# A token-major residual stream for a two-layer diffusion backbone: 512-column output products, a norm turned by a diagonal product, gates broadcast from DRAM

## The chip, the cores and the metric

The kernel runs on one core of a Trainium2 chip. The metric is the device time of one execution in microseconds (us), the median of several runs. Inputs and weights lie in DRAM; all weights, some 590 MB with the modulation matrices, are read once per execution.

## The reference, cut to what matters

Two groups of 128 tokens, a prompt and a latent sample, pass through two layers of width 2048 with the same weights. Each layer normalises and modulates its input, runs three mixers on one input projection, and adds the gated output projection; then it does the same with a SwiGLU feed-forward part. The modulation vectors come from a product of a condition vector with `w_mod`, per layer six of 2048 columns, and each group has its own. The change touches the norms, the two gated residual sums and the end.

```python
def rms_norm(x, g):
    y = x * lax.rsqrt(jnp.mean(x * x, axis=-1, keepdims=True) + EPS)
    return y * g

def trunk_layer(x, mod, lp, ctx=None):
    sh1, sc1, g1, sh2, sc2, g2 = [m[:, None] for m in jnp.split(mod, 6, axis=-1)]
    h = rms_norm(x, lp['ln_mix']) * (1.0 + sc1) + sh1
    u_hy, u_gla, u_mla = _split(h @ lp['w_in'], (HY_IN, GLA_IN, MLA_IN))
    ...
    y = jnp.concatenate([y_hy, y_gla, y_mla], axis=-1) @ lp['w_out']      # 2048 x 2048
    x = x + g1 * y
    h = rms_norm(x, lp['ln_ffn']) * (1.0 + sc2) + sh2
    gate, up = jnp.split(h @ lp['w_ffn_in'], 2, axis=-1)                  # 2048 x 2*5632
    x = x + g2 * ((jax.nn.silu(gate) * up) @ lp['w_ffn_out'])             # 5632 x 2048
    return x, ...

# both groups, layers 0 and 1, then
y_prompt, y_sample = rms_norm(x_ctx, ln_final), rms_norm(x_lat, ln_final)
```

## The kernel before, in words

**Products.** All large products run in a split form: every fp32 weight tile `w` of 128 rows and up to 1024 columns is rounded by ScalarE to a high part `wh` (`act`, L157) and VectorE makes the low part `wl = w - wh` (`tt`, L130); activations have a high and a low part too, and three products of TensorE (`mm`, L166) stand for one. `gemm_steps` walks over the row tiles of a weight; `weights` loads a tile on SP's DMA queue and splits it, one step ahead. A plan says what a step multiplies. A "w" entry (`plan_w`) holds a 128x128 piece of the weight still and moves the 256 tokens past it, so the result is feature-major: features on partitions, tokens along the columns. A "t" entry holds 128 tokens of the activation still and moves up to 512 weight columns past it, so the result is token-major. `w_in`, `w_out` and `w_ffn_out` use "w" entries (apart from two of the gated linear attention); `w_ffn_in` uses "t" entries. Four PSUM banks (`ps_g`) take the result. After the last `tail` row tiles, done bank by bank, `evict` drains each bank.

**The residual stream** `xT` is feature-major, 16 tiles of 128 features by 256 tokens. At the start x is loaded token-major and turned by 32 transposes. `residual` adds a bank into it with four VectorE operations of 128 columns (the gate of a feature is a per-partition number of `modv`). `SquareSum` squares two tiles at a time on ScalarE, adds most of them on VectorE and sums over partitions by products with a matrix of ones, the last ones right after the last banks. `rsq` turns that into the inverse root `rstd`, 256 columns wide on every partition. `norm_mod`'s `pre(k)` makes one tile of the normalised input, high and low, from `xT` and `rstd`; it is called in the step that uses tile k, so the mixer's first product (`c_a`) and the FFN's first product come with it. At the end `final_transpose` and `final_scale` turn x back and scale it.

**Order.** Tile's list scheduler orders each engine's instructions; program order is the priority. `w_mod` columns (`mods`) are computed beside the rest: layer 0's first two by TensorE in four quarters during the start (`mod_first`), others by `mod_pe` (TensorE) or `mod_dve` (VectorE sums `macc`, L295, ticked per product step). `early_load`/`early_run` put a few row tiles of the next modulation product into TensorE's waits at the end of `w_out` and of layer 0's `w_ffn_out`. VectorE's sums emitted after a product are ordered behind the last vector operation of its eviction (`dve["evict"]`).

**FFN.** Three segments of 16, 16 and 12 column tiles of 128. In a segment `w_ffn_in` runs gate, then up, for 8 (last segment: 6) column tiles at a time; `turn` transposes the result (L1210) and splits it into `ah`, `al`; then `w_ffn_out` runs twice, for 1024 output columns each (r = 0, 1). `w_out` runs twice in the same way.

## Time and profile before

| | us |
|---|---|
| median of 3 runs | 2466.58 (2464.02 to 2468.85) |
| the profiled execution | 2465.36 |
| its span, first to last instruction | 2463.3 |

| stage of the span | us | TensorE busy | VectorE busy |
|---|---|---|---|
| w_out, layer 0, until its modulation sums end (435 to 513) | 78.00 | 74.84 | 77.76 |
| FFN's first steps with the norm (543 to 591) | 48.00 | 48.00 | 47.87 |
| w_ffn_out, second segment, layer 0 (993 to 1085) | 92.00 | 92.00 | 83.59 |
| w_ffn_out, first segment, layer 1 (1878 to 1971) | 93.00 | 93.00 | 46.97 |

Matmuls overlap: an instruction's duration runs from its start to the end of its last column, and the next one starts long before that. The pace of TensorE is the distance of starts. An fp32 product (not the rounded form) leaves two records, a transpose one. TensorE's granted clock is 1.00 in all of these stages.

### The profile page before, as it was taken

The numbers are of one execution on the slowest core, as the hardware profiler recorded it, in microseconds if no ns is written. First come the engines' busy times: TensorE is split into PE (matmuls) and PEld (weight loads), VectorE is DVE, ScalarE is ACT, GpSimd is POOL, SyncE is SP. The second block draws the span as 40 slices with busy tenths as digits, with TensorE's granted clock in tenths as the row PEclk, the third lists the DMA queues.
The fourth block names the chain that finished last, engine by engine and source line by source line (L and its number), as shares of the span: only waits on it lengthen the run. The fifth ranks groups of instructions, "written<-read, shape, count | busy, mean of one in ns | idle before, by whom it ended". The sixth has DMA issues, their size and how long they took to land.

```text
span 2463.3 us, 39715 instructions
## 1 busy us (share of the span) xinstructions
PE 2400.4 (97%) x15925; PEld 2093.2 (85%) x15925; DVE 1725.8 (70%) x2439; ACT 1027.9 (42%) x1413; POOL 0.2 (0%) x4
## 2 busy tenths in 40 slices
PE   6899999999999999999999999999999999999998
PEld 3567777988889888999997888998888988899998
DVE  3565555988888978888988565698696555454555
ACT  2234342445433434434445444335443344434443
POOL 0000000000000000000000000000000000000000
PEclk9999999999999999999999999999999999999999
DMA  8988887877777878777876676586785666656662
GB/s 300 321 288 308 292 298 270 299 240 244 252 272 264 291 261 302 241 266 260 316 293 181 226 248 214 182 301 218 246 282 186 187 191 188 193 181 169 186 203 95
DMA packets 167276, 600.73 MB, mean 244 GB/s; under 512 B 18576, under 2 KB 24882, under 8 KB 146612
## 3 DMA queue, kind: packets, MB, share of 16 engines
q1 hardware_dynamic: 164104, 592.27, 71.4%
q10 hardware_dynamic: 2988, 5.93, 0.7%
q8 instruction: 125, 2.05, 0.3%
q14 instruction: 59, 0.48, 0.1%
HBM read 592.03 MB, written 6.09 MB: 243 GB/s over the span
## 4 chain that ended last, share of the span: by engine, by line
PE 90%; DMA 4%; DVE 4%; ACT 1%; issue 1%; SPq 0%; ACTq 0%; DVEq 0%
PE pg L166 77%; PE px L166 8%; DMA mw<-in_w_mod_dram 4%; PE mps L166 3%; DVE macc L295 2%; DVE wl L130 1%; PE px L1210 1%; DVE xT L135 0%; DVE sqa L130 0%; DMA w<-in_w_in_dram 0%; ACT e L157 0%; PE px L955 0%; ACT wh L157 0%; DVE nt L135 0%; PE px L984 0%
## 5 line engine op out<-in xcount | busy, mean ns | idle before, releaser
L157 ACT ACTIVATE wh<-w 128x1024 fp32r<-128x1024 f32 (+3 forms) x816 | 768.2, 950 | 1118.8 <-PE pg L166 931.7
L130 DVE TENSOR_TENSOR wl<-w,wh 128x1024 fp32r<-128x1024 f32 (+3 forms) x816 | 873.0, 1086 | 479.6 <-ACT wh L157 472.2
L166 PE MATMUL pg<-wh,hh 128*128 128x512 f32 (+1 forms) x1600 | 597.5, 374 | 1.1 <-DVE nt L135 1.1
L166 PE MATMUL pg<-wh,hl 128*128 128x512 f32 (+1 forms) x1600 | 596.0, 372 | 0.0
L166 PE MATMUL pg<-wl,hh 128*128 128x512 f32 (+1 forms) x1600 | 594.9, 372 | 0.0
L295 DVE SCALAR_TENSOR_TENSOR macc<-mw,sc,macc 128x1024 f32<-128x1024 f32 x324 | 402.0, 1280 | 0.0
L166 PE MATMUL pg<-ah,wh 128*128 128x256 f32 x1408 | 397.4, 283 | 0.0
L166 PE MATMUL pg<-al,wh 128*128 128x256 f32 x1408 | 396.3, 282 | 0.0
L166 PE MATMUL pg<-ah,wl 128*128 128x256 f32 x1408 | 395.4, 281 | 0.0
L166 PEld LDWEIGHTS pg<-wh,hh 128*128 128x128 f32 x1600 | 300.5, 188 | 45.0 <-ACT hh L157 2.9
L166 PEld LDWEIGHTS pg<-wl,hh 128*128 128x128 f32 x1600 | 300.5, 188 | 42.6
L166 PEld LDWEIGHTS pg<-wh,hl 128*128 128x128 f32 x1600 | 300.8, 188 | 41.2 <-issue 0.3
L166 PEld LDWEIGHTS pg<-ah,wh 128*128 128x128 f32 x1408 | 265.2, 189 | 1.8 <-issue 1.7
L166 PEld LDWEIGHTS pg<-al,wh 128*128 128x128 f32 x1408 | 265.7, 189 | 0.2
L166 PEld LDWEIGHTS pg<-ah,wl 128*128 128x128 f32 x1408 | 265.5, 189 | 0.1
L166 PE MATMUL pg<-hh,wh 128*128 128x256 f32 x832 | 245.0, 296 | 4.1 <-ACT hh L157 2.1
L166 PE MATMUL pg<-hl,wh 128*128 128x256 f32 x832 | 239.3, 289 | 0.0
L166 PE MATMUL pg<-hh,wl 128*128 128x256 f32 x832 | 236.2, 287 | 2.5 <-DVE wl L130 2.4
L166 PEld LDWEIGHTS pg<-hh,wh 128*128 128x128 f32 x832 | 159.7, 192 | 31.6 <-issue 19.5
L166 PEld LDWEIGHTS pg<-hl,wh 128*128 128x128 f32 x832 | 159.9, 192 | 10.0 <-issue 8.7
L166 PEld LDWEIGHTS pg<-hh,wl 128*128 128x128 f32 x832 | 158.6, 192 | 11.3 <-issue 6.3
L166 PE MATMUL mps<-mw,sc 128*32 128x256 f32 (+1 forms) x1024 | 113.8, 522 | 21.2 <-DMA mw<-in_w_mod_dram 21.0
(289 smaller groups left out, 2155.1 us busy)
## 6 DMA issues: line engine op xcount, KB each, us to landing
mw<-in_w_mod_dram SPq DMA_DIRECT2D x160, 1024.0 KB
w<-in_w_ffn_in_dram SPq DMA_DIRECT2D x256, 512.0 KB
w<-in_w_ffn_out_dram SPq DMA_DIRECT2D x176, 512.0 KB
w<-in_w_ffn_in_dram SPq DMA_DIRECT2D x128, 384.0 KB
mw<-in_w_mod_dram SPq DMA_DIRECT2D x64, 512.0 KB
w<-in_w_in_dram SPq DMA_DIRECT2D x64, 512.0 KB
w<-in_w_out_dram SPq DMA_DIRECT2D x64, 512.0 KB
w<-in_w_in_dram SPq DMA_DIRECT2D x64, 256.0 KB
```

Of the source, the lines that this page charges most:

```text
L130: r = nc.vector.tensor_tensor(out=out, in0=a, in1=b, op=op)
L157: r = nc.scalar.activation(out=out, in_=a, func=func, **k)
L166: r = nc.tensor.matmul(*args, **kw)
L295: r = nc.vector.scalar_tensor_tensor(out=acc[:, i, cs], in0=w[:, cs], scalar=c, in1=acc[:, i, cs], op0=ALU.mult, op1=ALU.add)
L1210: nc.tensor.transpose(p[:, j], s[:, 128 * j:128 * j + 128], ident)
```

## The change

The residual stream becomes `xt`, token-major: 128 tokens on partitions, 2048 features along the columns, one half per group. x is loaded straight into it.

- `w_out` and `w_ffn_out` use "t" entries: a step is 12 products of 512 columns (`plan_t`) and not 24 of 256. The last FFN segment takes 8 and then 4 column tiles; for the 4, gate and up share one product.
- `residual` multiplies a bank with the gate (`tt`, 512 columns) and adds it (`tt`). The gate must now lie along the columns, the same on all partitions: `mod_finish` transposes a finished gate, copies it to SBUF and stores it in DRAM on POOL's queue; `gate_load` reads it back with a partition broadcast, 2 x 512 KB ahead of each product.
- `square` sums squares along the columns by ScalarE's accumulator; `token_rms` turns them into one factor per token and a diagonal matrix `diag`.
- `norm_mod` multiplies a 128x128 tile of `xt` with `diag` (fp32, two products per k): that turns the tile and scales it at once. Scale and shift are applied on the way out of PSUM. `gemm_steps` calls `pre` one step ahead (`LOOK`).
- After `w_out` the early products are put ahead of the flush of the modulation sums.
- At the end no transposes: ln_final is read by partition broadcast and multiplied, and `scale_out` scales and sends each group.

```diff
+    def gate_load(l, m, r, pool, tags):
+        out = []
+        for g, tag in enumerate(tags):
+            t = pool.tile([128, 1024], F32, tag=tag, name="gb", bufs=1)
+            src = gates[l, m].rearrange("(g h k) c -> g h (k c)", g=2, h=2)[g, r]
+            nc.gpsimd.dma_start(t, src.partition_broadcast(128))
+            out.append(t)
+        return out
...
+    def square(pool, tag, g, j, bufs):
+        junk = pool.tile([128, 512], F32, tag=tag, name="junk", bufs=bufs)
+        act(junk, xt[:, g, 512 * j:512 * j + 512], AF.Square, accum_out=ssq[:, g, j:j + 1])
+
+    def token_rms(g, final=False):
+        m, r, t = (ssq[:, g, 4 + i:5 + i] for i in range(3))
+        nc.vector.tensor_reduce(out=m, in_=ssq[:, g, 0:4], axis=mybir.AxisListType.X, op=ALU.add)
+        ts(m, m, 1.0 / D, ALU.mult, EPS, ALU.add)
+        act(r, m, AF.Ln)
+        act(r, r, AF.Exp, scale=-0.5)
+        stt(t, m, r, r, ALU.mult, ALU.mult)
+        ts(t, t, -0.5, ALU.mult, 1.5, ALU.add)
+        if final:
+            tt(t, t, r, ALU.mult)
+            return t
+        ts(diag[:, g], ident, r, ALU.mult, t, ALU.mult)
...
         def pre(k):
+            p = px([128, 2, 128])
+            for g in range(2):
+                mm(p[:, g], xt[:, g, 128 * k:128 * k + 128], diag[:, g], start=(g == 0), stop=(g == 1))
             t = pool.tile([128, 256], F32, tag="nt", name="nt", bufs=2)
             for g in range(2):
                 s = slice(g * 128, g * 128 + 128)
-                b = modv[:, l, msh, k, g:g + 1]
-                stt(t[:, s], xT[:, k, s], modv[:, l, msc, k, g:g + 1], rstd[:, s], ALU.mult, ALU.mult)
-                act(hh[:, k, s], t[:, s], AF.Identity, bias=b)
-                stt(hl[:, k, s], t[:, s], b, hh[:, k, s].bitcast(F32), ALU.add, ALU.subtract)
+                c, b = modv[:, l, msc, k, g:g + 1], modv[:, l, msh, k, g:g + 1]
+                act(hh[:, k, s], p[:, g], AF.Identity, scale=c, bias=b)
+                ts(t[:, s], p[:, g], c, ALU.mult, b, ALU.add)
+            tt(hl[:, k], t, hh[:, k].bitcast(F32), ALU.subtract)
...
+    def residual(pool, tag, bufs, gb, b, r, bank, squares):
+        g, i = divmod(b, 2)
+        j = 2 * r + i
+        x = xt[:, g, 512 * j:512 * j + 512]
+        t = pool.tile([128, 512], F32, tag=tag, name="rt", bufs=bufs)
+        tt(t, bank, gb[g][:, 512 * i:512 * i + 512], ALU.mult)
+        tt(x, x, t, ALU.add)
+        if squares:
+            square(pool, tag, g, j, bufs)
+        return g, j
...
+    plan_t = [(2 * t + i, 0, 512, f"t{t}", 512 * i) for t in range(2) for i in range(2)]
...
-                gemm([T["w_out"][l][:, 1024 * r:1024 * r + 1024]], k_tiles(order), yT, plan_w(8), ev_out, tail=1 + r, quiet=QUIET * r,
+                gemm([T["w_out"][l][:, 1024 * r:1024 * r + 1024]], k_tiles(order), yT, plan_t, ev_out, tail=1 + r, quiet=QUIET * r,
                      done=(lambda: early_run(l, 5, range(1), pe["last"])) if r else None)
+            early_run(l, 5, range(1, EARLY), pe["last"])
             mod_flush((l, 3))
-            early_run(l, 5, range(1, EARLY), pe["last"])
-            rsq(rstd, ss.ps, ss.acc[:, 0:256])
...
-                    n = 8 if nkt == 16 else 6
+                    n = min(8, nkt - done_kt)
...
+                    if n == 8:
+                        run_late(gemm_steps([w_gate], k_tiles(range(KT)), hT, plan, ev_gate_ff, pre=pre, quiet=16 if pre else 0))
+                        run_late(gemm_steps([w_up], k_tiles(range(KT)), hT, plan, ev_up))
+                    else:
+                        run_late(gemm_steps([w_gate, w_up], k_tiles(range(KT)), hT, plan, ev_both))
```

## Rows read from the trace of the kernel before

**Rows 1.** The page: busy time of each engine; shares of the chain that ended last.
```profile
PE 2400.4 (97%) x15925; PEld 2093.2 (85%) x15925; DVE 1725.8 (70%) x2439; ACT 1027.9 (42%) x1413; POOL 0.2 (0%) x4
...
PE 90%; DMA 4%; DVE 4%; ACT 1%; issue 1%; SPq 0%; ACTq 0%; DVEq 0%
```
**Rows 2.** Timeline of TensorE, w_ffn_in and w_ffn_out: start us, us, instruction, count.
```profile
654.64 0.39 PE L166 MATMUL pg<-wh,hh 128*128 128x512 f32 x1
...
656.90 0.39 PE L166 MATMUL pg<-wh,hl 128*128 128x512 f32 x1
...
1039.74 0.28 PE L166 MATMUL pg<-al,wh 128*128 128x256 f32 x1
...
1041.50 0.28 PE L166 MATMUL pg<-al,wh 128*128 128x256 f32 x1
```
**Rows 3.** Chain in order of time, FFN of layer 0: start us, us, what, count.
```profile
639.54 2.76 PE pg L166 x12
...
1002.20 0.44 PE px L1210 x4
1002.64 2.82 PE pg L166 x24
...
1160.76 2.09 PE pg L166 x12
```
**Rows 4.** Timeline of TensorE, fp32 products of 128 columns in the Hyena mixer.
```profile
395.95 0.39 PE L166 MATMUL px<-mats,yim 128*128 128x128 f32 x2
...
396.85 0.39 PE L166 MATMUL px<-mats,yim 128*128 128x128 f32 x2
```
**Rows 5.** Stretches: us, each engine's busy (instructions), granted clock, DMA share, GB/s.
```profile
435.00:513.00 78.00, 74.84 (x617) 72.70 (x616) 77.76 (x91) 33.49 (x37) 0.00 (x0) 1.00 0.85 306
...
543.00:591.00 48.00, 48.00 (x212) 39.72 (x213) 47.87 (x89) 29.79 (x52) 0.00 (x0) 1.00 0.65 210
993.00:1085.00 92.00, 92.00 (x786) 91.96 (x785) 83.59 (x95) 35.08 (x36) 0.00 (x0) 1.00 0.77 264
...
1878.00:1971.00 93.00, 93.00 (x789) 92.61 (x782) 46.97 (x61) 34.84 (x35) 0.00 (x0) 1.00 0.58 181
45.00:60.00 15.00, 12.89 (x111) 9.12 (x110) 8.47 (x29) 6.12 (x17) 0.00 (x0) 0.92 0.76 257
```
**Rows 6.** Chain, from w_out to the FFN in layer 0.
```profile
534.50 5.23 PE px L166 x20
...
542.99 3.04 PE pg L166 x12
```
**Rows 7.** Chain, from layer 0's w_ffn_out to layer 1.
```profile
1294.15 1.12 DVE xT L135 x4
1295.27 4.79 DVE macc L295 x4
...
1301.17 3.41 PE mps L166 x26
```
**Rows 8.** Chain, the first norm of layer 0.
```profile
44.06 3.62 PE px L166 x8
...
51.17 1.93 PE pg L166 x12
```
**Rows 9.** Chain, the end.
```profile
2449.23 0.44 PE px L984 x4
...
2456.48 1.33 DVE yt L140 x2
```
**Rows 10.** Squares of x: ns min/median/max, first and last start us, shapes.
```profile
L157 ACT ACTIVATE sq<-xT x35: 613/630/636, 37.8 to 2451.8; 128x512 f32<-128x512 f32 x35
...
L130 DVE TENSOR_TENSOR sqa<-sqa,sq x22: 649/692/695, 38.4 to 2444.4; 128x512 f32<-128x512 f32 x22
```
**Rows 11.** One-column operations of the attention's softmax, same columns.
```profile
L157 ACT ACTIVATION_READ_ACCUMULATOR e<-px,st x32: 192/204/217, 216.9 to 1445.5; 128x1 f32 x32
L140 DVE TENSOR_SCALAR st<-st x16: 158/162/171, 216.2 to 1444.2; 128x2 f32<-128x2 f32 x16
```

More of the change, by code (lines that the diff above doesn't have):

```diff
@@ L40 @@
 EARLY = 4
+LOOK = 1
 FF_RATE = 0.252
@@ L235, in mod_finish @@
         mods_done.add((l, m))
+        if m in (2, 5):
+            p = px([32, 128])
+            nc.tensor.transpose(p, modv[:, l, m].rearrange("p k g -> p (k g)"), ident)
+            row = mp.tile([32, 128], F32, tag="mtr", name="row", bufs=1)
+            act(row, p)
+            gates[l, m] = dram.tile([32, 128], F32, name=f"gate{l}{m}")
+            nc.gpsimd.dma_start(gates[l, m], row)
     def mod_load(l, m, kt, pool):
@@ L384, in gemm_steps @@
         for ti, (row, kt) in enumerate(tiles):
+            if pre is not None:
+                for i in range(0 if ti == 0 else ti + LOOK, min(ti + LOOK + 1, nt)):
+                    pre(tiles[i][1])
             fetch(ti + 1)
             wh, wl = ahead.pop(0)
-            if pre is not None:
-                pre(kt)
             a, c = x(kt)
@@ L558, in tile_backbone @@
         nc.vector.tensor_copy(out=v2T, in_=p[:, :at])
[L560 to L581 removed]
+        for g, nm in enumerate(("x_prompt", "x_sample")):
+            for half in range(2):
+                cs = slice(half * 1024, half * 1024 + 1024)
+                nc.scalar.dma_start(xt[:, g, cs], T[nm][0, :, cs])
+        for g in range(2):
+            for j in range(4):
+                square(pool, "junk", g, j, 2)
+            token_rms(g)
     def hyena_filters(pool, l):
@@ L812, in gla @@
             p = px([128, 2, 2, 128])
-            mm(p, ones[:, 3], sq, start=True, stop=True)
+            mm(p, ones[:, 2], sq, start=True, stop=True)
             rsq(sq, p, og[:, g].rearrange("p (i j) t -> p i j t", i=2))
@@ L1205, in turn @@
                             halves[half] = ah, al
[L1206 to L1209 removed]
+                            parts.extend((ah[:, j], al[:, j]) for j in range(4))
+                        ah, al = (v[:, :, 128 * t:128 * t + 128] for v in halves[half])
+                        p = px([128, 4, 128])
+                        for j in range(4):
                             nc.tensor.transpose(p[:, j], s[:, 128 * j:128 * j + 128], ident)
@@ L1243, in tile_backbone @@
                         early_load(l + 1, 4)
-                    run_late(gemm_steps([T["w_ffn_out"][l][:, 1024 * r:1024 * r + 1024]], tiles, aT, plan_w(8), ev_ff, tail=2 if last_seg and r else 1,
+                    run_late(gemm_steps([T["w_ffn_out"][l][:, 1024 * r:1024 * r + 1024]], tiles, aT, plan_t, ev_ff, tail=2 if last_seg and r else 1,
                          quiet=QUIET if nxt else 0,
```

154 lines of the change are left out of this document (45 added, 109 removed).

## Prediction

> **What bounds the kernel now.** I read the page's engine totals and its chain first. TensorE is busy 97% of the span and 90% of the chain that ended last lies on it [rows 1], so what counts is TensorE's issue time, stage by stage, and then the few places where TensorE waits. Busy durations mislead here, because matmuls overlap, so I took starts from the timeline: ten 512-column products of w_ffn_in start 2.26 us apart in all, 0.226 each, and fifteen 256-column products of w_ffn_out 1.76 us apart, 0.117 each [rows 2]. Two 256-column products cost 0.235, one 512-column product 0.226: the half-width form is only some 4% dearer, although its recorded duration is 0.28 against 0.39. The chain in order of time says the same with small additions: 24 narrow products in 2.82, 12 wide ones in 2.76, 12 of 384 columns in 2.09 [rows 3].
>
> The table of stretches then shows who limits each stage [rows 5]. In w_out (435 to 513) VectorE is busy 77.76 of 78 us: there TensorE waits for VectorE. In w_ffn_out of layer 0 VectorE has 83.59 of 92 us, near the limit; in layer 1 only 46.97 of 93.
>
> **The change part by part.** All sums are made against the profiled execution (2465.36 us, span 2463.3; it is 1.22 below the median of the runs).
>
> *w_ffn_out, wide.* 44 row tiles x 2 column halves x 2 layers = 176 steps, each 24 narrow products before and 12 wide ones after. A step now: the stretch 993 to 1085 holds 32 steps and four groups of transposes at 0.44 [rows 3], (92 - 1.8)/32 = 2.82; 1878 to 1971 gives (93 - 1.8)/32 = 2.85 [rows 5]. Mean 2.835. After: 12 x 0.226 to 0.227 = 2.72. 176 x 0.115 = 20 us less. The low end is the chain's pair, 2.82 against 2.76, 176 x 0.06 = 10.6; I take 20, because the pieces of the chain begin and end at transposes and the stretches don't. [...] Each bank is now drained by two 512-element tensor_tensor (0.69 recorded, [rows 10]) in place of four 128-element operations (1.12 for four, [rows 7]): 0.25 us more per bank, on VectorE, beside the next product. For layer 0, where VectorE has 8 us of slack in 92 and TensorE takes away 4, I charge 2 us. Net -18.
>
> *w_ffn_in's last segment.* Four products of 16 steps x 12 x 384 columns become three of 16 x 12 x 512: 64 x 2.09 = 133.8 against 48 x 2.74 = 131.5 [rows 2, 3]. -2.3 per layer, -4.6.
>
> *w_out.* Until 513 VectorE decides, and what it does there is mostly weight splitting and the modulation sums, both unchanged. Its drain of four banks goes from 1.12 + 0.62 (the sum of squares moves away) to 1.3: -1.8 us. Past 513 seven steps are left at -0.115: -0.8. One ones-product group (0.9) leaves TensorE. -3.5 per layer; the gate copies add 2 MB to a stage whose DMA share is already 0.85 [rows 5], which I charge with 1 us (0 to 3, if they displace weight loads one for one). -2.5 per layer, -5.
>
> *Norm by a diagonal product.* This is the added cost. Each of 16 k needs two fp32 products of 128 columns. The nearest row is in the Hyena inverse transform: fp32 128x128 products start 0.22 us apart, and each appears as two records [rows 4]. 16 x 2 x 0.223 = 7.1 us per norm, 7.4 with the change of operand type around it. Before, the norm had nothing on TensorE. In both FFN norms and in layer 1's mixer norm the products that follow are limited by TensorE, so three norms are paid in full: +22. The look-ahead of one step hides the ScalarE and VectorE part, not this. From below: if TensorE had waits there to fill it would be less, but in 543 to 591, the norm's stretch, TensorE is busy 48.00 of 48 us [rows 5], so I exclude a gain.
>
> *Layer 0's start and mixer norm.* The x transposes go (hidden anyway). The chain from the sum of squares to the first product is ones-product 3.62, then rstd and norm until 51.17 [rows 8]; after it, squares and row factors can be ready as soon as x lands, and the first product waits for the modulation columns at about 44.1, so it starts some 5 us earlier. Bytes bound the stage: DMA runs at 257 GB/s in 45 to 60 [rows 5], so an earlier start can fill that hole. I take -3.5 (0 to -6), and +3 for the diagonal products where the four quarters are not bound by bytes (0 to 7). Net -0.5.
>
> *w_out to FFN.* Now 8.5 us pass from 534.50 to the first product at 542.99 [rows 6], of which 5.23 is ones-products interleaved with early modulation products. After: two tensor_tensor 1.3, square 0.63 plus accumulator read 0.20 [rows 10, 11], five one-column operations at 0.16 to 0.2 with their hops 1.5, the diagonal 0.3, two fp32 products 0.6, ScalarE and the low part 1.2, about 6. The early products, put ahead of the flush, fill TensorE meanwhile. -2.5 each (0 to -4), -5.
>
> *w_ffn_out to layer 1.* The last modulation sums (four, 4.79 [rows 7]) are held until the last vector operation of the eviction. That was the residual; it becomes the correction inside the row factor, behind square, Ln and Exp: 2.2 us later, and 1301.17's early products still follow those sums. One group of ones-products (1.0) goes. +1.2.
>
> *The end.* From the last product at 2449.2 to the end are 14 us: transposes, ones-products, four scalings, the last two from 2456.48, then the output's flight [rows 9]. After: group 0 is finished and sent while group 1 is still computed; VectorE has three 0.62 operations per bank and one 0.69 scaling per group from about 4 us before the last product, 10 us in all, so it ends near +6.3, plus flight 4.5, 10.8 in place of 14. About 3 us of transposes and ones-products between the last w_ffn_out products also go. -6.5 (-2 to -9).
>
> *Gate path.* Per gate one transpose, one copy, one small store and 1 MB read back through POOL's queue, which is empty now. The reads are issued one product (45 us) ahead of their use; a 1 MB move at the 264 GB/s of [rows 5] takes 4 us. Nothing, with that cover; if the cover were gone, 4 us per product, 16 products.
>
> Sum: -18 - 4.6 - 5 + 22 - 0.5 - 5 + 1.2 - 6.5 = -16.4: 2465.4 to 2449 for the profiled execution, 2450 for the median.
>
> **The rivals.**
> A, slower: VectorE takes the place of TensorE as the bound in layer 0. For: 83.59 of 92 busy, and 77.76 of 78 in w_out [rows 5]. It decides once a w_ffn_out stretch needs more VectorE time than the 88.5 us that TensorE will need; 83.6 + 8 x 0.25 = 85.6 is under it, but the sums come in blocks of 4.8 us. Then layer 0's gain of 10, the 5 of w_out and the 5 of the transitions are lost and the start gives nothing (3.5): +7, 2473.
> B, no change: the wide products give only what the pieces of the chain show, 10.6 in place of 20 [rows 3], and the small-operation chains at the transitions cost what they save (5), as they cross between engines more often than the old ones. -16.4 + 9.4 + 5 = -2, 2464. For it: the pieces are what the end is made of; against it: the stretches. [...]
> C, slower: a gate read lands late, for instance held up by VectorE or queued behind weights, the bank is not drained and the next product waits. 4 us x 16 products is 64 at worst, 2513; a third of that, if only some land late, gives -16.4 + 21 = +5, 2470. Against it: 45 us of cover. [...]
> D, faster: the fp32 products slip into small waits (3 us less per norm, 9) and the transitions gain what their bounds allow (5 more): -30, 2435. For it: TensorE waits at both ends of each norm's stretch; against it: the full stretch of [rows 5].
>
> **How the numbers follow.** The forecast (2441 to 2460) gets 0.52, A 0.12, B 0.13, C 0.05, D 0.18. A measurement of this kernel can tell about 0.2%, 4.9 us. Faster by more than that: 0.48 of the forecast, D, and a little of B: 0.68. Same: most of B and the rim of the forecast: 0.15. Slower: A and C: 0.17. The range from 2434 to 2471 leaves out half of A and C and the far part of D.
>
> **What would show it.** Right: the products of w_ffn_out start 0.226 to 0.227 apart and a step takes 2.72; each norm's 16 steps are 0.45 longer on TensorE, with 64 records of fp32 128x128; VectorE stays full in w_out and its end moves by only 3 us; the gap before the FFN is about 6 us and that at the end about 11. Wrong: wide products at other than 0.227 in this orientation; TensorE waiting for wl in layer 0's w_ffn_out (A); a tensor_tensor on gb released by a DMA (C); weight loads late in w_out; or the list-scheduled order of the untouched mixer stage coming out differently, which I can't price from this trace.

## The result and the profile after

The changed kernel takes 2491.9 us (median of 4 runs, 2489.1 to 2498.7) against 2467.7 for the kernel before: ratio 1.0105, 95% interval 1.008 to 1.0129. It is 1% slower, where 2450 was forecast; 2492 lies outside the range of 2434 to 2471. The profiled execution has 2490.35 us with a span of 2488.6, so 25 us more than the one before, where 16 less had been summed up.

The first view is the table of stretches of the changed kernel, for the first norm of the FFN in layer 0 and one w_ffn_out stage of each layer; columns as in [rows 5].

```profile
551.00:599.00 48.00, 47.39 (x221) 38.52 (x221) 34.80 (x60) 26.33 (x44) 0.00 (x0) 0.94 0.43 127
1015.00:1095.00 80.00, 80.00 (x352) 64.51 (x351) 75.06 (x71) 31.56 (x32) 1.05 (x2) 1.00 0.82 289
1916.00:2006.00 90.00, 90.00 (x396) 72.45 (x395) 45.63 (x47) 34.98 (x36) 2.64 (x5) 1.00 0.65 214
```

TensorE is still the limit of w_ffn_out in both layers; VectorE has 75.06 of 80 us in layer 0, so it is not full (rival A), and no bank waits for a gate read (rival C). New is the clock: 0.94 in the norm's stretch, which had 1.00 in [rows 5].

Where the 25 us come from is read from the starts of the first products of each stage on TensorE's timeline:

| part | before, us | after, us | difference | forecast |
|---|---|---|---|---|
| layer 0's start and quarters, to the next mixer stage | 255.94 | 265.74 | +9.8 | -0.5 |
| w_out, two layers | 99.43, 99.42 | 97.16, 97.48 | -4.2 | -5 |
| w_out to FFN, two layers | 8.52, 8.53 | 8.65, 8.35 | -0.1 | -5 |
| three norms that TensorE bounds | 176.4, 176.4, 38.5 | 186.9, 186.4, 49.6 | +31.5 | +22 |
| w_ffn_out, first two segments, two layers | 94.0, 92.1, 93.1, 93.1 | 92.0, 91.9, 92.0, 91.9 | -4.5 | -13 |
| w_ffn_out, last segments (with what left TensorE there) | 72.4, 74.3 | 68.5, 68.5 | -9.8 | -9 |
| w_ffn_in, last segments | 136.6, 134.6 | 134.7, 132.5 | -3.9 | -4.6 |
| w_ffn_out to layer 1 | 10.5 | 19.6 | +9.1 | +2.2 |
| last product to the end | 14.1 | 12.9 | -1.2 | -3.3 |
| rest of the mixers | | | -1.5 | 0 |

(The forecast's terms are laid into these rows; the norms of the FFN stand as the stretch from the first w_ffn_in product of the first segment to the end of its last.) Four rows carry the miss: the start, the norms, w_ffn_out and the way to layer 1; a fifth, w_out to FFN, gave nothing where 5 us had been forecast.

### The profile page after: what moved, and what is told of

The parts are those of the page before. It is cut to its first block, busy times and chain, and to the rows that moved or that the text cites. A ratio compares the mean times of both kernels' runs of the same rounds, so it can differ in the third digit from the quotient of the medians.

```text
span 2488.6 us, 33219 instructions
## 1 busy us (share of the span) xinstructions
PE 2406.0 (97%) x12769; PEld 1914.5 (77%) x12769; DVE 1722.8 (69%) x2213; ACT 1027.0 (41%) x1409; POOL 19.9 (1%) x41
## 4 chain that ended last, share of the span: by engine, by line
PE 88%; DVE 6%; DMA 4%; ACT 2%; issue 1%; ACTq 0%; SPq 0%; DVEq 0%
PE pg L167 74%; PE px L167 9%; PE mps L167 4%; DVE macc L319 3%; DMA mw<-in_w_mod_dram 2%; DVE wl L131 1%; PE px L1210 1%; ACT wh L158 1%; DMA w<-in_w_out_dram 1%; DVE xt L131 0%; DMA fw<-in_hy_filt_w_dram 0%; DMA w<-in_w_in_dram 0%; ACT junk L158 0%; PE px L955 0%; ACT hh L158 0%
## 5 line engine op out<-in xcount | busy, mean ns | idle before, releaser
L158 ACT ACTIVATE wh<-w 128x1024 fp32r<-128x1024 f32 (+2 forms) x784 | 760.7, 980 | 1094.9 <-PE pg L167 876.5
L131 DVE TENSOR_TENSOR wl<-w,wh 128x1024 fp32r<-128x1024 f32 (+2 forms) x784 | 869.2, 1123 | 470.6 <-ACT wh L158 466.9
L167 PE MATMUL pg<-wh,hl 128*128 128x512 f32 x1472 | 576.4, 392 | 1.0 <-DVE hl L131 0.9
L167 PE MATMUL pg<-wh,hh 128*128 128x512 f32 x1472 | 575.3, 395 | 0.7 <-ACT hh L158 0.5
L167 PE MATMUL pg<-wl,hh 128*128 128x512 f32 x1472 | 573.3, 390 | 0.0
L167 PE MATMUL pg<-wh,ah 128*128 128x512 f32 x704 | 281.0, 399 | 0.0
L167 PE MATMUL pg<-wh,al 128*128 128x512 f32 x704 | 278.9, 396 | 0.0
L167 PE MATMUL pg<-wl,ah 128*128 128x512 f32 x704 | 277.5, 396 | 0.0
L167 PEld LDWEIGHTS pg<-wh,ah 128*128 128x128 f32 x704 | 132.6, 188 | 33.3 <-issue 1.7
L167 PEld LDWEIGHTS pg<-wl,ah 128*128 128x128 f32 x704 | 132.6, 188 | 32.4
L167 PEld LDWEIGHTS pg<-wh,al 128*128 128x128 f32 x704 | 132.6, 188 | 31.2
```

What stands on the lines that cost most here:

```text
L131: r = nc.vector.tensor_tensor(out=out, in0=a, in1=b, op=op)
L158: r = nc.scalar.activation(out=out, in_=a, func=func, **k)
L167: r = nc.tensor.matmul(*args, **kw)
```

## The experiments

**1. Why are wide products slow in w_ffn_out alone?** TensorE's timeline of the changed kernel, w_ffn_out of layer 0 (start us, us, instruction, count):

```profile
1030.37 0.40 PE L167 MATMUL pg<-wl,ah 128*128 128x512 f32 x1
...
1033.18 0.39 PE L167 MATMUL pg<-wl,ah 128*128 128x512 f32 x1
```

and its chain in the same stage (transposes, then one step; `pg` is the bank of a large product, `px` a small PSUM buffer):

```profile
1018.96 0.44 PE px L1210 x4
1019.39 2.80 PE pg L167 x12
1022.19 0.44 PE px L1210 x4
```

Twelve products in 2.81 us, 0.234 each, against 0.226 for the same form in w_ffn_in [rows 2]; a step of 2.80 is next to the 2.82 of 24 narrow ones [rows 3]. Most of the gain of the width is gone, and nobody waits for anything. In w_out the wide products keep 0.227.

e1_pace, the data of the operands `ah`, `al` exchanged for those of `hh`, `hl`, the normalised input that w_ffn_in reads; in layer 1 `hh` and `hl` are read where they lie, and the products keep their shape and number:

```diff
-                        act(ah, p)
-                        tt(al, p, ah.bitcast(F32), ALU.subtract)
+                        act(ah, normed["hh"][:, k0:k0 + 4, ...])
+                        nc.vector.tensor_copy(out=al, in_=normed["hl"][:, k0:k0 + 4, ...])
...
-                    return parts[k]
+                    return hT(k) if l else parts[k]
```

> The changed kernel with other data in the operand of w_ffn_out. In layer 0 the tiles ah and al stay where they are, but are filled with columns of the normalised input (hh, hl) instead of the turned activation; in layer 1 w_ffn_out reads hh and hl themselves and ah and al are not read. The products computed are therefore wrong ones of the same shape and number. It separates why the 512-column products of w_ffn_out start 234 ns apart (230 to 238, uneven) where those of w_ffn_in with the same weights tiles start 226 to 227 apart. Theory values: the numbers in ah and al decide; then both layers come down to 226 to 227 ns and a step of twelve to 2.72 us. Rival place: the tiles' place or shape in SBUF decides; then layer 0 stays at 234 and layer 1 falls to 227. Rival weights: it is the w_ffn_out weights or their stream; then both layers stay at 234.

Layer 0: 234.1 to 234.2 ns with the other data. Layer 1, from hh and hl: 227.2. So it is neither the values nor the weights, but something of the tiles ah and al themselves: their place or their shape.

e5_align, a first guess at the place (the offsets here and below are those of the program's memory plan):

```diff
                     gb = gate_load(l, 5, r, fp, ("gb0", "gb1"))
+                    if f0 == 0 and r == 0:
+                        nc.vector.memset(fp.tile([128, 8], F32, name="pad"), 0.0)
```

> The changed kernel with one unused tile of 32 bytes per partition in the FFN pool, so that ah and al begin 32 bytes lower, at a multiple of 64 bytes in each partition (171968 in place of 172000), as hh, hl and the operands of w_out do already. The first run (operand data exchanged) pointed at the place of ah and al. Theory alignment: w_ffn_out's 512-column products fall from 234 to 227 ns, a step from 2.81 to 2.72, 176 x 0.085 to 0.09 = 15 us less in the sum of the w_ffn_out stages and about 2477. Rival region: what counts is that ah and al lie among the tiles that VectorE and the gate copies use, or their shape; then the products stay at 234 and the time within 3 us of the changed kernel.

233.3 in place of 234.1, 2493.6 us. A multiple of 64 bytes is not the point; the guess fell.

e8_narrow, the width undone in layer 1, with the shift of e5:

```diff
+    plan_n = [(2 * t + i, 256 * h, 256, f"t{t}", 512 * i + 256 * h) for t in range(2) for i in range(2) for h in range(2)]
...
-                    run_late(gemm_steps([...], tiles, aT, plan_t, ev_ff, ...
+                    run_late(gemm_steps([...], tiles, aT, plan_n if l else plan_t, ev_ff, ...
```

> The changed kernel with ah and al at a multiple of 64 bytes, and in layer 1 alone w_out and w_ffn_out cut into products of 256 columns in the new orientation (24 per step instead of 12, the same arithmetic). It measures what the width alone is worth in w_ffn_out, layer 0 (wide) against layer 1 (narrow) of the same run. Theory: 512 columns 226 to 227 ns against 256 columns 117 to 120, so a step is 2.72 against 2.81 to 2.88, as the prediction put it. Rival stream: both forms move the same columns at the same pace, 2 x 113.5 = 227, and width was worth nothing; then layer 1's steps take 2.72 too. Rival loads: twice as many weight loads of 128 columns are not hidden behind 256 columns in this orientation, and narrow costs over 125 each.

Layer 1's narrow products in w_ffn_out start 113.6 to 115.6 ns apart, its stages take 91.0, 89.5 and 66.8 us; layer 0's, with wide ones, take 91.7, 91.5 and 68.2. In w_out of the same run it is the other way: 120 narrow, 227 wide. So it isn't the width either: the pace of each form changes with the tiles it reads.

e9_micro, the cost by itself: nothing but the triples of products, at chosen byte offsets of the two operands in the partition.

> Not the kernel but the disputed cost alone: nothing of the reference is computed, constant operands, the high/low triples of the kernel in three forms: t512 and t256 (activation tile as the stationary operand, 512 or 256 columns of weights moving) and w (128 columns of weights stationary, 256 columns of activation moving). Each with the stationary and the moving operand at 0, 32, 64 or 96 bytes past a multiple of 128 in the partition, four steps of 12 or 24 products each; the whole series once beside copies on ScalarE and subtractions on VectorE and once with these engines idle. Theory place: the pace hangs on the offset of the two operands; the series shows 227 for some pairs and 233 to 238 for others (t512), 113 to 120 for t256 and w. [...]

TensorE's timeline of that series, second half (the name says form, offset s of the stationary and m of the moving operand; the pace is the distance to the next start over the count):

```profile
687.90 11.41 PE L157 MATMUL qt512s96m0x<-W,A 128*128 128x512 f32 x48
699.15 11.36 PE L157 MATMUL qt512s96m32x<-W,A 128*128 128x512 f32 x48
...
721.55 11.07 PE L157 MATMUL qt512s96m96x<-W,A 128*128 128x512 f32 x48
732.46 11.67 PE L157 MATMUL qt256s0m0x<-W,A 128*128 128x256 f32 x96
...
823.58 11.05 PE L157 MATMUL qt256s64m0x<-W,A 128*128 128x256 f32 x96
834.47 11.52 PE L157 MATMUL qt256s64m32x<-W,A 128*128 128x256 f32 x96
845.83 11.68 PE L157 MATMUL qt256s64m64x<-W,A 128*128 128x256 f32 x96
857.34 2.88 PE L157 MATMUL qt256s64m96x<-W,A 128*128 128x256 f32 x23
```

(699.15 - 687.90)/48 = 234.4 ns for the changed kernel's pair, 96 and 0; (732.46 - 721.55)/48 = 227.3 where both lie alike, the change of form included. For 256 columns (834.47 - 823.58)/96 = 113.4 at 64 and 0, but 119.9 where both lie alike. All pairs, mean distance in ns without the first two of each group, 512 / 256 columns:

| stationary at | moving 0 | 32 | 64 | 96 |
|---|---|---|---|---|
| 0 | 227.4 / 119.9 | 233.4 / 117.8 | 228.9 / 117.8 | 233.6 / 119.9 |
| 32 | 233.2 / 118.3 | 226.7 / 119.9 | 233.4 / 117.8 | 228.9 / 117.8 |
| 64 | 233.3 / 113.3 | 233.2 / 118.3 | 227.0 / 119.9 | 233.4 / 117.8 |
| 96 | 234.4 / 118.7 | 233.3 / 117.8 | 233.2 / 118.3 | 226.9 / 119.9 |

The half beside a busy ScalarE and VectorE gives the same numbers to 0.1 (but for its very first group), so the traffic of these engines is out. With weights stationary (form w) the 256-column numbers return to 0.1. Theory place holds; no pair came under 226.7 for 512 columns and 113.3 for 256.

e13_align128, the proof in the kernel: the pad made 96 bytes, so that ah and al lie as wh and wl do.

> The changed kernel with an unused tile of 96 bytes in the FFN pool, so that ah and al begin at a multiple of 128 bytes, the same offset as the weights wh and wl. In the isolated series 512-column products took 234.4 ns with the stationary operand at 96 and the moving one at 0 (the changed kernel), 233.3 at 64 and 0 (the shift of 32 bytes that was tried), and 226.7 to 227.4 where both have the same offset. Theory: the products of w_ffn_out fall from 234 to 227, its stages from 92.0 and 68.5 us to 88.9 and 66.3, in all 16 us less, about 2475. Rival: in the kernel something else about these tiles counts, the series only looks alike; then 233 to 234 as before, and 2490.

TensorE's timeline of that kernel, same stage:

```profile
1030.32 0.39 PE L167 MATMUL pg<-wl,ah 128*128 128x512 f32 x1
...
1033.04 0.39 PE L167 MATMUL pg<-wl,ah 128*128 128x512 f32 x1
```

2.72 for twelve, 2476.3 us (1.0047, 1.0031 to 1.0064), the six stages 14.3 us shorter (89.5, 89.2, 66.5, 89.5, 89.3, 66.4). One unused tile gives back 15.6 of the 24 us (14.3 by the six stages).

**2. The way to layer 1.** The chain of the changed kernel, from the end of the last w_ffn_out product of layer 0 (1304.75) to layer 1's first (start us, us, what, count; `macc` is a modulation sum, `mps` the bank of the modulation products on TensorE):

```profile
1307.71 0.60 DVE xt L131
...
1310.40 0.22 DVE ssq L136
1310.62 1.20 DVE macc L319
...
1313.33 1.21 DVE macc L319
1314.54 0.14 issue
1314.67 3.50 PE px L167 x16
1318.18 1.69 PE mps L167 x10
...
1324.45 0.55 PE pg L167 x3
```

The four held modulation sums (4.79 in one piece at 1295.27 in [rows 7]) now start at 1310.6, 5.9 us after the end of the last product where it was 1.3, behind the first operation of the row factor's correction (`ssq` L136), and share VectorE with the rest of it. TensorE's timeline is empty from 1305.7, where eight early products end, to 1314.67. Then it works at a granted clock of 0.50 (1314.6 to 1316.4) and 0.58 (to 1318.2), before it has 1.00 again. The sums' products are 16 records in 3.50 us there; in the chain of the kernel before, 8 of them are left:

```profile
1300.11 1.06 PE px L166 x8
```

e2_early_first:

```diff
-            mod_flush(*ffd)
             if l < DEPTH - 1:
                 early_run(l + 1, 4, range(1, EARLY), pe["last"])
+            mod_flush(*ffd)
```

> The changed kernel with the early modulation products of layer 1 put ahead of the flush of the modulation sums at the end of layer 0, as the change already does at w_out. Theory: the 19.6 us from the last w_ffn_out product of layer 0 to the first product of layer 1 (10.5 before the change) are long because TensorE has nothing in its order between 1305.2 and 1314.7 but the products that wait for the last four modulation sums; the early products then fill this hole, 3.4 us at full clock, and the clock does not fall, 4 us more: 7 to 8 us less in all, about 2484. Rival: the chain from the last sums through the sel products, the transpose and the norm sets the first product of layer 1, and the early products were hidden or in nobody's way: within 2 us of the changed kernel.

The gap stays at 20.3, the time is 2493.2, as the rival had it. TensorE's timeline of that run shows two reasons, where the rival named one:

```profile
1325.95 3.39 PE L167 MATMUL px<-macc,sel 128*32 128x512 f32 x16 [5.49 <-DVE macc L319]
1331.17 1.07 PE L167 MATMUL mps<-mw,sc 128*32 128x512 f32 x8 [1.83 <-DMA mw<-in_w_mod_dram]
```

The sums set the end of the hole, 9.9 us after the last product (1316.03) as in the changed kernel, and their products take 3.39. Behind them, where the early products had stood, come eight later modulation products, which wait for their load. So filling the hole doesn't end it sooner; what the way would take without that load is not shown.

e11_rate:

```diff
-FF_RATE = 0.252
+FF_RATE = 0.27
```

> The changed kernel with the modulation sums in the FFN dealt out a little faster (0.27 steps per weight tile in place of 0.252), so that those of layer 0 are all done inside its w_ffn_out and none is held behind the last eviction. Theory: the 19.6 us between the last w_ffn_out product of layer 0 and the first product of layer 1 are set by the four last sums, which wait for the correction of the row factor, then by their products, a transpose and the norm; without them the gap is that of the row factors alone, about 10 to 12 us, and some 2 us of the sums' products come back inside w_ffn_out. Rival: the chain of row factors with its interleaved weight splits is as long by itself; then the gap stays over 17.

Its chain over the same gap:

```profile
1307.22 3.57 PE mps L167 x32
1310.79 0.87 PE px L167 x6
...
1313.11 1.51 ACT hh L158 x4
...
1314.67 0.63 PE pg L167 x3
```

7.5 us from 1307.22 to 1314.67 in place of 19.6, less than the kernel before had. The norm behind it takes 46.9 instead of 49.6. The clock has no part in that, it is 1.00 in both stretches; but fewer modulation products lie among the norm's (the work on `mw`, the modulation weights, first in the changed kernel, then in e11: stretch, busy us and records of TensorE, its weight loads and VectorE, granted clock, DMA share, GB/s):

```profile
1324.40:1374.00 49.60, 3.21 (x15) 0.43 (x12) 0.00 (x0) 1.00 0.58 171
1314.67:1361.60 46.93, 1.04 (x2) 0.14 (x2) 0.00 (x0) 1.00 0.62 191
```

The sums' products cost 2.1 and 2.2 us in two w_ffn_out stages and leave 2.2 in the w_ffn_in between them. One run: 2478.8 us.

**3. Layer 0's start.** e3_look0:

```diff
-{"pre": norm, "pieces": dup}
+{"pre": norm, "pieces": dup, "look": 0}
...
-            gemm(c_a, order, hT, plan_a, ev_a, pre=norm, pieces=dup)
+            gemm(c_a, order, hT, plan_a, ev_a, pre=norm, pieces=dup, look=l)
```

> The changed kernel without the look-ahead of the norm in layer 0's mixer (each step's diagonal products are issued in their own step, not one step ahead; layer 1 and the FFN keep it). Theory: the diagonal products made a step ahead hold the three small PSUM buffers that the Hyena filters of layer 0 also need, so that the filters' chain, and with it the quarter products around it, is stretched: quarters 2 and 3 took 105 us in place of 85. Without it layer 0's four quarters come back by 8 to 11 us, about 2482. Rival bytes: the quarters are bound by the weight loads that were given another order; then it stays within 3 us. Rival cover: without look-ahead each of 16 steps waits for the norm's chain of diagonal product, ScalarE and VectorE, about 1.2 us; then layer 0 is up to 10 us longer, some 2500.

2500.4 us, and the stage behind the quarters begins at 278.7; nine runs with the changed kernel's start have 265.7 to 275.6 there. The look-ahead wasn't it, and its cover was worth some 9 us by the medians. But the trace of that run showed that the filters' first product comes no earlier (100.4). That product (ns min/median/max, first and last start us) in the kernel before,

```profile
L166 PE MATMUL px<-fzt,fw x4: 269/294/320, 57.8 to 115.1; 33*64 33x128 f32 x4
```

in the changed kernel,

```profile
L167 PE MATMUL px<-fzt,fw x4: 269/294/320, 96.5 to 154.6; 33*64 33x128 f32 x4
```

and with e6_fq0 (`FQ = 1` made `FQ = 0`, which also brings the table of constants forward by a quarter):

```profile
L167 PE MATMUL px<-fzt,fw x4: 268/294/320, 58.7 to 110.4; 33*64 33x128 f32 x4
```

> The changed kernel with the Hyena filters of both layers called one quarter earlier in the program (after the first and second quarter of layer 0's mixer instead of after the second and third). Theory ring: the three small PSUM buffers are handed out in the order of the program, and the norm's diagonal products now stand in that ring ahead of the filters; the filters' first product came at 57.8 before the change and at 96.5 after it, and quarters 2 and 3 are stretched by the filters' chain that then has nothing to hide behind. Called one quarter earlier, the filters start by about 60 again and the first product of quarter 4 comes 8 to 14 us earlier (189.8 in the changed kernel), total about 2481. Rival bytes: the start is bound by weight loads or by the modulation columns, whatever the filters do; then quarter 4 starts within 3 us of 189.8 to 198 and the time is that of the changed kernel.

The filters begin at 58.7, as the theory of the ring has it. It isn't their data: in the changed kernel the loads for that product and for the table were issued by 41.0, and 96.5 comes behind the norm's last product for the second quarter (91.9). Quarter 4 begins at 185.7 instead of 189.8, and quarters 1 and 2 later (48.3 instead of 44.4, 99.8 instead of 84.5), behind the filters' buffers.

What that is worth is less clear. The next stage begins at 261.9, but its start no longer marks the same work: of the attention's four groups of products three begin ahead of it in the changed kernel, and two in e6. Attention's products in the changed kernel and in e6:

```profile
L167 PE MATMUL px<-kn,qn x32: 270/327/382, 225.2 to 282.0; 128*128 128x128 f32 x16, 128*128 128x256 f32 x16
L167 PE MATMUL px<-kn,qn x32: 270/326/382, 224.2 to 286.4; 128*128 128x128 f32 x16, 128*128 128x256 f32 x16
```

They end 4.4 us later, and w_out begins at 446.2, in the nine runs at 444.8 to 456.1 (445.5 in the changed kernel), in the kernel before at 435.0. The median is 2485.5 us, 6.4 less, but the runs (2478.6 to 2490.3) touch those of the changed kernel, and the profiled one is the slowest of them. So the ring is shown as the reason for the late filters, and not as the reason for the 9.8 us.

**4. The norms.** e12_warm:

```diff
             early_run(l, 5, range(1, EARLY), pe["last"])
+            p, after = px([128, 512]), pe["last"]
+            for i in range(3):
+                r = mm(p, ident, mats[:, 4 * i:4 * i + 4], start=True, stop=True)
+                tc.add_manual_dep(r.ins, after, no_sync, reason="order")
             mod_flush((l, 3))
```

> The changed kernel with three idle products of 512 fp32 columns put behind the early modulation products between w_out and the FFN, where TensorE otherwise stands still for most of 546.2 to 551.3. Theory clock: TensorE's clock falls to 0.50 right behind this pause (549.9 to 556.7 in layer 0, 1727.5 to 1730.9 in layer 1) because of it; with the pause filled it stays at 1.0, and each FFN's first segment gets 2 to 3.5 us shorter. Rival: the fall has its cause earlier or elsewhere, the clock falls as before, and the stretch keeps its 186 to 187 us or grows by the added products.

The stretches of the changed kernel,

```profile
543.00:550.00 7.00, 3.97 (x37) 1.36 (x29) 5.74 (x15) 4.50 (x12) 0.00 (x0) 0.99 0.50 153
550.00:557.00 7.00, 6.88 (x22) 5.50 (x23) 3.86 (x11) 3.85 (x9) 0.00 (x0) 0.52 0.01 2
```

and of this one:

```profile
543.00:550.00 7.00, 6.59 (x41) 2.72 (x34) 5.47 (x15) 4.50 (x12) 0.00 (x0) 1.00 0.50 152
550.00:557.00 7.00, 6.47 (x34) 5.01 (x33) 5.49 (x13) 4.58 (x10) 0.00 (x0) 1.00 0.01 2
```

TensorE is busy 6.59 of 7 us instead of 3.97 and the clock stays; the norm's stretch falls from 186.9 and 186.4 to 184.7 and 184.9. So 2.2 and 1.5 us of the 10 are the clock's, about as expected in layer 0 and less in layer 1. With the clock at 1.00 (550.7 to 598) the price of the diagonal products can be read from the same timeline:

```profile
586.30 0.61 PE L167 MATMUL px<-diag,xt 128*128 128x128 f32 x4
...
589.57 0.61 PE L167 MATMUL px<-diag,xt 128*128 128x128 f32 x4
```

A step of twelve products with one tile's four records takes 3.27 us; without them it is 2.72 to 2.76 [rows 2, 3].

e10_transpose prices the product itself, in the two FFN norms:

```diff
-                mm(p[:, g], xt[:, g, 128 * k:128 * k + 128], diag[:, g], start=(g == 0), stop=(g == 1))
+                nc.tensor.transpose(p[:, g], xt[:, g, 128 * k:128 * k + 128], diag[:, g])
...
-        ts(diag[:, g], ident, r, ALU.mult, t, ALU.mult)
+        ts(diag[:, g], ident, t, ALU.mult, 0.0, ALU.is_gt)
```

> The changed kernel with the tiles of the two FFN norms turned by a plain transpose instead of the diagonal product; the row factor is left out there, the wait for the chain of row factors is kept. It prices the diagonal product. The FFN norms' stretch, from the first w_ffn_in product to the end of that segment, took 186.9 and 186.4 us against 176.4 before. Theory, the prediction's term: two records 0.22 us apart against one of 0.11, so 3.5 us less per FFN norm, 183.3. Rival clock: the larger part of the 10 us is the half clock after the gap, and the transposes leave TensorE idle for longer; then 185 or more.

184.8 and 183.1, so 2.1 and 3.2 us for half the records, beside a clock that falls as before (0.94 in 553.3 to 601, 0.94 in 551 to 599 of the changed kernel); doubled, 4 and 6 us. By the steps it is 0.5 us a tile, 7 us for the 14 tiles of the stretch (two are made ahead of it), so the term of 7.4 is about right. Of the 10 us about 7 are the products and 2 the clock; the last is waiting at single places (for one, 0.49 us for `hl` at 592 in e12) and stands in no experiment.

e7_prescale:

```diff
-                mm(p[:, g], xt[:, g, 128 * k:128 * k + 128], diag[:, g], start=(g == 0), stop=(g == 1))
+                nc.gpsimd.tensor_scalar(out=xs[:, g], in0=xt[:, g, 128 * k:128 * k + 128], scalar1=ssq[:, g, 6:7], ...)
+                nc.tensor.transpose(p[:, g], xs[:, g], ident)
```

> The changed kernel with the norm tiles turned by a transpose instead of a product with the diagonal of row factors: the row factor is applied before it, by a one-column multiplication on GpSimd, which is idle. It computes the reference's result. Theory, by the step of the prediction: a diagonal product is two records 0.22 us apart, a transpose one of 0.11; 16 x 2 x 0.11 = 3.5 us less in each of the three norms that TensorE bounds, 10 to 11 in all, about 2481. Rival GpSimd: two multiplications of 128 columns and the hop take longer than a step's 2.7 us, or they hold VectorE; then the norms get longer instead, 16 x 0.5 = 8 us each, some 2515. Rival clock: the norms' excess is mostly the half clock after the gap, which stays; then the gain is under 4 us.

```profile
L494 POOL TENSOR_SCALAR xs<-xt,ssq x128: 592/603/1787, 34.0 to 1787.6; 128x128 f32<-128x128 f32 x128
```

0.60 us each, and with one buffer for both groups GpSimd begins only when the transposes before it are done (25.6 us of waiting for them in 558 to 602); the norms take 188.4, 187.1 and 56.1, the kernel 2500.2 us. Rival GpSimd, in this form with one buffer.

**5. One part alone.** e4_before_split84, in the kernel before:

```diff
-                    n = 8 if nkt == 16 else 6
+                    n = min(8, nkt - done_kt)
...
+                    else:
+                        run_late(gemm_steps([w_gate, w_up], k_tiles(range(KT)), hT, plan, ev_both))
```

> The kernel before with one part of the change alone: the last segment of w_ffn_in as one product of 8 tiles and one of 4 (gate and up in one product) in place of four products of 384 columns. Theory, as the prediction has it: 64 steps of 2.09 become 48 of 2.74, 2.3 us less per layer, 4.6 in all, about 2463. Rival: the joined product loads its weights as two pieces of 256 KB per step and leaves fewer steps behind which the last turns are done, which gives the gain back: within 1 us of the kernel before.

The two stages take 134.7 and 132.6 us instead of 136.6 and 134.6, 1.9 each; the total, 0.9994 (0.9976 to 1.0013), can't tell 4 us from none.

**6. Do the causes add up?** e14_mended has the edits of e13, e11, e6 and e12 together.

> The changed kernel with the four causes taken away together: ah and al at the offset of the weights, the modulation sums done before the end of layer 0's FFN, the filters called one quarter earlier, and three idle products in the pause before each FFN. Theory, the causes add up: 2492 less 16 (w_ffn_out), 13 (gap to layer 1), 7 (layer 0's start) and 4 (clock) gives about 2452, near what the prediction had for the change. Rival: they overlap, or there is another loss that none of them names; then it stays over 2460.

2455.9 us, 0.9963 (0.9949 to 0.9978): 36 of the expected 40 us come back, and the kernel is 0.4% faster than the one before. The start is short of its part: in the profiled execution w_out begins at 443.3, 2 us earlier than in the changed kernel, where 7 were expected. The forecast is 6 us further; 5 us of it are the term w_out to FFN, which none of these edits touches.

**7. Is the gain the change's, or the places'?** e15_before_off, in the kernel before:

```diff
-            normed[t] = nh.tile([128, KT, 256], F32R, tag=t, name=t)
+            normed[t] = nh.tile([128, KT * 256 + 32], F32R, tag=t, name=t)[:, o:o + KT * 256].rearrange(...)
...
-        new_h()
+        new_h(16 if msc == 1 else 0)
...
+            nc.vector.memset(ym.tile([128, 16], F32, name="ypad"), 0.0)
...
+                        nc.vector.memset(fp.tile([128, 16 if l else 24], F32, name="pad"), 0.0)
```

> The kernel before, with nothing of the change: only the tiles' places are shifted by 32 to 128 bytes, so that in every 256-column product the stationary weights lie at 64 and the moving operand at 0 past a multiple of 128 (113.3 ns in the isolated series, where equal offsets gave 119.9), and in w_ffn_in's products both at the same offset (227 as now). Theory: w_ffn_out's six stages fall to 88.8 and 67 us, 25 us less in all, the mixers' products by 6.5 ns each, some 1800 of them where TensorE is the limit, 8 us (0 to 12), w_out past its VectorE-bound part 2 us: about 2430. Rival: in the stages VectorE or the weight loads take over and most of the gain becomes waiting; then over 2450.

2468.0 (1.0009 to 1.0034), a miss: 117.8 in w_ffn_out and w_out, and 231 in w_ffn_in, where the two distances next to a product with hl were 232 to 234 and the third 227. Counted past a multiple of 256, hl lay 128 bytes off from wh there and hh did not; and in w_ffn_out the weights lay at 64 and the moving tiles at 128, 64 apart the wrong way round (0 and 64 in the series: 117.8). The series had only tried offsets up to 96. Its twin, e16_mended_off, carried the same fault into the mended kernel:

> The mended changed kernel with the same shift in the mixers: weights at 64, the mixers' hh and hl at 0, everything that is stationary against 512 moving columns at 64. Theory: as the mended one with 8 us (0 to 12) less in the mixers, about 2444; against the kernel before with shifted tiles it decides whether the change is worth something once both have the right places: the wide form has then nothing left to win in w_ffn_out (12 x 227 against 24 x 113.3), and the diagonal products cost 22 us, so the kernel before should be the faster of the two by about 10. Rival: the wide form keeps an advantage by fewer instructions, and this one is as fast or faster.

2471.3; w_ffn_in again at 231. The question stayed open until both were placed by multiples of 256 (hh alone longer and seen at 64 or 128 bytes into it, a pad of 192 bytes ahead of ymh; in the mended kernel hh and hl 256 bytes longer):

> The kernel before with the tiles shifted once more, now counted past a multiple of 256 bytes. The first shift gave 117.8 where 113.3 was expected, and 231 in w_ffn_in where 227 was; there hh and hl lay 128 bytes apart in that count, which the isolated series (offsets up to 96) never had. Now w_out and w_ffn_out have stationary weights at 192 and the moving operand at 128, the mixers the same for hh (hl stays at 192), and w_ffn_in everything at 192. Theory: 113.3 ns in w_ffn_out and past the VectorE-bound part of w_out, 115.5 in the mixers, 227 in w_ffn_in: w_ffn_out's six stages 25 us less, mixers 0 to 8, w_out 2, about 2433. Rival: the pair 192 and 128 is not the pair 64 and 0, products stay at 117 to 118 and the time over 2450.

```profile
1000.33 0.28 PE L166 MATMUL pg<-ah,wl 128*128 128x256 f32 x1
...
1001.35 0.28 PE L166 MATMUL pg<-ah,wl 128*128 128x256 f32 x1
```

(TensorE's timeline of e17, w_ffn_out of layer 0.) Nine narrow products in 1.02 us, 113 each. The four first stages of w_ffn_out take 89.2 to 89.3 us, what the wide form takes at its best (e13: 89.2 to 89.5); w_ffn_in keeps 227, the mixers only reach 118. 2442.9 us, 0.9915 (0.9898 to 0.9932): nothing of the change in it, and the fastest kernel of the study.

> The mended changed kernel with the mixers' tiles shifted, counted past a multiple of 256 bytes: weights at 192 everywhere, hh and hl at 128 in the mixers and at 192 in the FFN, the operands of w_out and w_ffn_out at 192. Theory: 113.3 ns in the mixers, 227 in all wide products, some 8 us (0 to 12) under the mended kernel, about 2447; the kernel before with its shifted tiles is then the faster of the two by some 10 us, since the wide form has nothing left to win and the diagonal products stay. Rival: no gain in the mixers, whose stretches wait for VectorE and the weights; then 2454 to 2457.

2451.6 (0.9935 to 0.9966), 4 us under e14 in place of 8, and 9 over e17. With the places chosen on both sides, the change, mended as in e14, costs 9 us; the runs of the two don't overlap (2435.2 to 2445.9 against 2448.5 to 2453.6).

## Why the prediction was wrong, step by step

*w_ffn_out, wide* is the step that was wrong in its mechanism and cost most (14.3 us, e13): -20 was taken from 0.226 to 0.227 of w_ffn_in [rows 2]. That row has the same form of instruction but other tiles. At the places which the change's memory plan gave ah and al the product takes 234, and the 4% between two halves and a whole in [rows 2] was a difference of places: at the best place of each, 24 x 113.4 = 2.72 and 12 x 227.4 = 2.73. So joining two halves saves nothing by itself; e13 and e17, with 89.2 to 89.5 us for a stage of wide products and 89.2 to 89.3 for one of narrow ones, show the same. Some 6 us came of it (4.5 in the first two segments, 128 of the 176 steps), because the tiles before lay badly too, with 117 to 120 ns; the chain's 10.6 would have been nearer but not right either. With the pad of e13 the six stages are even 28.6 us shorter than before, where 22 had been laid into these rows: that, too, is what the places happened to be.

*Norm by a diagonal product.* Right in kind and nearly in size (7.4; about 7 for the records). Missing was 1.5 to 2.2 us per FFN norm (e12) at a granted clock of 0.50 (549.9 to 556.7, and 1727.5 to 1730.9 in layer 1): the early products, on which the text counted as a filling, end at 546.2, a first tile takes 0.7 us at 547.8, the next follow at 549.9, and the text did not ask what the pause does to the clock (with it filled, 1.00 in e12). In layer 1's mixer norm 2.7 of 11.1 are mostly modulation products that the longer way pushed into it, as e11 shows.

*w_out to FFN.* The chain was summed as if VectorE had only this to do. It is interleaved with two weight splits of the next stage, 1.2 us each (chain of the changed kernel):

```profile
542.90 1.23 DVE wl L131
...
546.13 0.60 DVE rt L131
...
549.54 0.36 DVE diag L143
...
551.28 2.16 PE pg L167 x4
```

The last bank's product with the gate runs at 546.1 though the bank was done at 542.6. 8.65 us in place of 6. No run took the splits out of the way, so their share is read, not shown.

*w_ffn_out to layer 1.* The mechanism was named (the sums wait for the correction inside the row factor) but priced at 2.2; they start 4.6 later. That their products, all 16 records in one piece and at a granted clock of 0.50 to 0.58, take 3.50 where 1.06 were left, and that early products and the norm's follow one after the other (6.3 from there to the first product, 3.4 before), made it 9.

*Layer 0's start* was costed by bytes and by TensorE, and it is the largest miss of a row (+9.8 where -0.5 was forecast). The first product did come earlier (44.4 against 51.2), but the norm's new use of three small PSUM buffers put it ahead of the filters in their ring, and they began 39 us later. The prediction named "the list-scheduled order of the untouched mixer stage" as what it could not price, and the order did change; how much of the 9.8 that is stays open, as e6 won nothing at w_out's first product.

Right: w_out (-4.2 for -5), the last segment of w_ffn_in (-3.9 for -4.6, alone again in e4), VectorE and the gate path as hidden work, and, with the last segments of w_ffn_out, the end. The rivals: A and C did not occur; B's first half did (some 6 from the width, less than 10.6), for another reason than B's, and with losses that no rival had.

Open: why an offset matters at all; the 118.6 ns of the kernel before in layer 1's w_ffn_out (a pair 128 bytes apart, which the series lacks) and its 117.4 to 119.7 in layer 0's; the reason for the 10 us of the start.

## What to carry to other kernels

A pace read from one stage holds for that stage's tiles (here 0.226 us in w_ffn_in and 0.234 in w_ffn_out): before a change of form is priced by a row of another stage, compare the two stages' paces in the form that both have, and where they differ without a wait, look at the byte offsets of the operands. A new user of a shared ring of buffers takes its turn in program order; list who stood behind it (here the filters, 39 us). Whatever moves the last operation of an eviction moves everything that is ordered behind it. A mark like "the first product of the next stage" measures a gain only if the same work lies ahead of it in both runs.

## What the runs showed of the hardware

In e9 the distance of two fp32r products changed with where stationary and moving operand lie in the partition: 226.7 to 234.4 ns for 512 columns, 113.3 to 119.9 for 256, with the same instruction, no wait and a granted clock of 1.00. Equal offsets gave the lowest numbers for 512 columns (226.7 to 227.4) and 119.9, the highest, for 256. In the table the 512-column numbers go by the distance of the two offsets (the moving one 32 ahead 233.4, 64 ahead 228.9, 32 behind 233.2), the 256-column ones don't (113.3 for 64 and 0, 117.8 for 96 and 32). Offsets counted past 128 bytes did not tell the pace in e15 (117.8 where 113.3 was expected); counted past a multiple of 256 the pairs 64 and 0 (e9), and 192 and 128 (e17), gave 113.3 to 113.6 for 256 columns.

Two fp32 products of 128x128 between fp32r products of 512 columns cost 0.5 us (e12, a step of 3.27 against 2.72 to 2.76). In front of the FFN's norm of the changed kernel TensorE was busy 3.97 of 7 us, and its granted clock was 0.52 in the 7 us behind; with 6.59 of 7 it stayed at 1.00 (e12).
